# Output matmuls of a chunked S5 scan: swapping the stationary and the moving operand, on four column strips

## Chip, cores and metric

The kernel runs on one core of one Trainium2 chip. The metric is the device time of one execution in microseconds: 1356.96 us before the change, the median of three runs (1354.83 to 1357.64).

## What is computed

Two identical layers of a decoder trunk over 256 tokens of 1024 channels. Each layer has a gated feed-forward half-step, three token mixers that share one input projection, a gated merge, and a second feed-forward half-step. The change touches mixer B, an S5 layer: 32 groups of 16 channels, each with 64 complex states.

```python
def s5_layer(u, lam_re, lam_im, log_dt, b_re, b_im, c_re, c_im, d_skip):
    ...
    lam_bar = jnp.exp(lam * dt)
    b_bar = ((lam_bar - 1.0) / lam)[:, :, None] * b
    bu = jnp.einsum('gpc,bsgc->bsgp', b_bar, u32.astype(jnp.complex64))
    ...
    _, states = lax.associative_scan(combine, (a, bu), axis=1)
    y = jnp.einsum('gcp,bsgp->bsgc', c, states).real + d_skip * u32
    ...
y_b = jax.nn.gelu(s5_layer(...))
y_b = (y_b @ s5_glu_a[l]) * jax.nn.sigmoid(y_b @ s5_glu_b[l])
```

## The kernel before

**The whole.** Activations lie on 128 partitions, in two tiles of 128 tokens. Weights stream from HBM in units of 512 KB (`raw`, issued on SP at L210); ScalarE rounds each to a high part `wh` (L221), and DVE or GpSimd makes the low part `wl` from the rest (L228, L230). Each projection is three matmuls per block on these parts (`mm3`, L106 to L108), which I call wide matmuls: 128x128 stationary, 256 columns moving. A layer is one feed-forward, `mix1`, `mix2`, one feed-forward.

**What sets the order.** The program is written as one stream; the tile framework's scheduler sorts each engine's instructions by priority and by a simulated timeline, so instructions of several steps are mixed on an engine. At run time each engine works through its own list in order. `mix1` steps three Python generators in turn: `gA` (sparse attention), `gC` (dilated attention) and `gS`, the S5 layer, in between the projections.

**The S5 part.** The 256 tokens are cut into 32 chunks of eight. The 32 groups are handled in four quarters of eight groups. For a quarter q:

- `ahead(q)` and `late(q)` load what the setup (`setup_s5_layer`, during the feed-forward before) left in DRAM: `At`, the tables `tab`, the chunk inputs `U`; and `Gt` (from chunk state to outputs, L904) and `Tt` (from inputs of a chunk to its outputs, L907).
- `enter(q)` makes the chunk states: eight matmuls (L922), a rotation, a scan over the chunks on DVE (L931), a rotation back. Its last step (L937) leaves the states in `v`, 128 partitions (64 real and 64 imaginary parts) by 8 groups x 32 chunks.
- `leave(q)` makes the outputs of a quarter in one PSUM tile `yT` (tag `y`): eight matmuls of `Tt` with `U` (L944) and eight of `Gt` with the states one chunk back (L946). `Tt` and `Gt`, 128x128 per group, are the stationary operand, the 32 chunks of a group the moving one. The result stands with (position in the chunk, channel) on the 128 partitions and (group, chunk) along the columns.
- Then follows what I call the tail: Square on ScalarE (L950), two DVE operations (L951, L952), Tanh (L953), a DVE operation that makes `t1` (L954), the high part `yo` by a copy on ScalarE (L955), the low part on DVE (L956). Eight writes to DRAM (`yd`, L958, on SP) and two reads (`back`, L963) bring it to the layout that `mix2` multiplies.

L922, L944 and L946 are fp32 matmuls; the trace shows two records for each that is written. In the setup, L614 and L616 make the kernel tables `Kd` with stationary operands of 32 columns that write to 32 partitions each:

```python
for part in range(2):
    for a in range(4):
        ...
        o = pk[32 * a:32 * a + 32, 128 * s:128 * s + 128]
        ...
            PE.matmul(o[:, 16:], lh, h4[:, g, 0:7].rearrange("p n c -> p (n c)"), start=True, stop=True)
```

Attention brings transposes (L820, the 128x128 identity stationary) and matmuls with 64 stationary columns (L849, L874) into the same stage.

Of the kernel before, what the change touches and what calls it, by code (L numbers as in the profile page):

```python
# [23 lines left out]
F32 = mybir.dt.float32  # L24
F32R = mybir.dt.float32r
BF16 = mybir.dt.bfloat16
AF = mybir.ActivationFunctionType
ALU = mybir.AluOpType
AX = mybir.AxisListType

P = 128
# [41 lines left out]
def _body(ctx, tc, nc, I, out, depth, dbg):  # L73
# [7 lines left out]
    def sb(shape, dt, tag, bufs=1):  # L81
        cnt[0] += 1
        return pool.tile(shape, dt, name=f"{tag}_{cnt[0]}", tag=tag, bufs=bufs)

    def tb(shape, dt, tag, bufs=1):
        cnt[0] += 1
        return scope[-1].tile(shape, dt, name=f"{tag}_{cnt[0]}", tag=tag, bufs=bufs)
# [11 lines left out]
    def ps(tag):  # L99
        cnt[0] += 1  # L100
        return psum.tile([P, 1024 if tag == "sc" else 512], F32, name=f"{tag}_{cnt[0]}", tag=tag, bufs=PB[tag])

    V, A, G, PE = nc.vector, nc.scalar, nc.gpsimd, nc.tensor
# [10 lines left out]
    ident = sb([P, P], F32, "ident")  # L114
# [580 lines left out]
    def mix1(l, h, big, yAh, yAl, yGh, yGl):  # L695
# [48 lines left out]
        for t in range(2):  # L744
# [12 lines left out]
            for i in range(2):  # L757
# [4 lines left out]
            g = gqk[:, l:l + 1]  # L762
            A.activation(kk2[:, 0, tks[t]], pt[:, 0:P], AF.Copy, scale=g)
            V.scalar_tensor_tensor(kk2[:, 1, tks[t]], pt[:, 0:P], g, kk2[:, 0, tks[t]].bitcast(F32),
                                   op0=ALU.mult, op1=ALU.subtract)
# [132 lines left out]

        def s5():
            st = {}  # L900

            def late(q):
                Gt, Tt = tb([P, 8, 128], F32, "s5G"), tb([P, 8, 128], F32, "s5T")
                nc.sync.dma_start(Gt.rearrange("p g e -> p (g e)"), Gd[:, q])  # L904
                kq = Kd[8 * q:8 * q + 8]
                for r in range(8):
                    nc.sync.dma_start(Tt[r::8], kq[:, :, r:r + 8, :].rearrange("g x n c -> x g (n c)"))  # L907
                return Gt, Tt

            nxt = {}  # L910

            def ahead(q):
                nxt[q] = sb([P, 1024], F32, "x0"), tb([P, 3, 256], F32, "tab"), tb([P, 8, 32], F32, "s5U", 2)
                nc.sync.dma_start(nxt[q][0], Ad[:, q])
                nc.sync.dma_start(nxt[q][1], td[:, q])
                nc.sync.dma_start(nxt[q][2], ud[q].rearrange("(g c) (r k) -> (c r) g k", c=16, r=8))

            def enter(q):
                At, tab, U = nxt.pop(q)
                bu = ps("p2")  # L920
                for g in range(8):
                    PE.matmul(bu[:, 32 * g:32 * g + 32], At[:, P * g:P * g + P], U[:, g], start=True, stop=True)  # L922
                X = bu[:, :256]
                sw = tb([P, 256], F32, "s5sw")
                for e in range(2):
                    A.activation(sw[hps[e]], X[hps[1 - e]], AF.Copy)
                v, w = tb([P, 256], F32, "s5v", 2), tb([P, 256], F32, "s5w", 2)
                V.tensor_tensor(v, X, tab[:, 0], op=ALU.mult)
                V.tensor_tensor(w, sw, tab[:, 1], op=ALU.mult)
                V.tensor_tensor(v, v, w, op=ALU.subtract)  # L930
                V.tensor_tensor_scan(v, tab[:, 2], v, 0.0, op0=ALU.mult, op1=ALU.add)  # L931
                sw = tb([P, 256], F32, "s5sw")
                for e in range(2):
                    A.activation(sw[hps[e]], v[hps[1 - e]], AF.Copy)
                V.tensor_tensor(v, v, tab[:, 0], op=ALU.mult)
                V.tensor_tensor(w, sw, tab[:, 1], op=ALU.mult)
                V.tensor_tensor(v, v, w, op=ALU.add)  # L937
                st[q] = U, v

            def leave(q, Gt, Tt):  # L940
                U, v = st.pop(q)
                yT = ps("y")
                for g in range(8):
                    PE.matmul(yT[:, 32 * g:32 * g + 32], Tt[:, g], U[:, g], start=g == 0, stop=False)  # L944
                for g in range(8):
                    PE.matmul(yT[:, 32 * g + 1:32 * g + 32], Gt[:, g], v[:, 32 * g:32 * g + 31], start=False, stop=g == 7)  # L946
                yv = yT[:, :256]
                t1 = tb([P, 256], F32, "s5w", 2)
                yo = tb([P, 2, 256], F32R, "s5y")
                A.activation(t1, yv, AF.Square)  # L950
                V.tensor_scalar(t1, t1, 0.044715, 1.0, op0=ALU.mult, op1=ALU.add)  # L951
                V.tensor_tensor(t1, yv, t1, op=ALU.mult)  # L952
                A.activation(t1, t1, AF.Tanh, scale=math.sqrt(2 / math.pi))  # L953
                V.scalar_tensor_tensor(t1, t1, 1.0, yv, op0=ALU.add, op1=ALU.mult)  # L954
                A.activation(yo[:, 0], t1, AF.Copy, scale=0.5)  # L955
                V.scalar_tensor_tensor(yo[:, 1], t1, 0.5, yo[:, 0].bitcast(F32), op0=ALU.mult, op1=ALU.subtract)  # L956
                for r in range(8):
                    nc.sync.dma_start(yd[q].rearrange("i (g c) (r k) -> r c (i g) k", c=16, r=8)[r],  # L958
                                      yo[16 * r:16 * r + 16].bitcast(F32).rearrange("p i (g k) -> p (i g) k", k=32))

            def back(q):
                for i, a in enumerate((yGh, yGl)):
                    nc.sync.dma_start(a[:, q].bitcast(F32), yd[q, i])  # L963

            ahead(0)
            GT = late(0)
            for q in range(5):
                if q < 4:
                    enter(q)
                    yield  # L970
                if q > 0:
                    leave(q - 1, *GT)
                if q < 3:
                    ahead(q + 1)
                if q > 0:
                    if q < 4:
                        GT = late(q)
                    if q > 1:
                        back(q - 2)
                    yield  # L980
            back(3)
# [10 lines left out]
        gA = piped([(0, 0), (1, 0), (1, 1)], A1, A2)  # L992
        gC = attn_C()
        gS = s5()

        steps = iter([1, 0, 1, 0, 1, 0] + [1, 0, 1] + [1, 0, 1, 0, 1, 0, 1, 0] + [1] * 4)
# [143 lines left out]
    with Phase():  # L1140
        table(AF.Silu)
        with tc.high_priority():
# [5 lines left out]
            g = tb([P, D], F32, "G", 1)  # L1148
# [67 lines left out]
```

## Time and profile before

| | |
|---|---|
| median of three runs | 1356.96 us |
| the profiled execution | 1357.2 us |
| its span in the trace | 1355.4 us |
| TensorE busy | 1331.6 us (98%) |
| DVE, ScalarE, GpSimd busy | 826.8, 699.8, 465.3 us |
| mean granted clock of TensorE | 0.996 |
| DMA | 265.68 MB, 196 GB/s |

The span is the time between the first and the last instruction of the profiled execution; the rest of its 1357.2 us lies around it. Busy time of TensorE is counted from records whose ends are modelled and which overlap; where one matmul follows another, the distance of their starts is the cost. The feed-forwards fill more than half of the span; `mix1` lies from about 222 to 440 us in layer 0 and from about 890 to 1108 us in layer 1. The `leave` calls of layer 0 stand at 294 to 298, 332 to 337, 360 to 365 and 379 to 385 us, and those of layer 1 at 963, 1001, 1029 and 1048 us.

### The profile page before, as it was taken

The numbers are of one execution on the slowest core, as the hardware profiler recorded it, in microseconds if no ns is written. First come the engines' busy times: TensorE is split into PE (matmuls) and PEld (weight loads), VectorE is DVE, ScalarE is ACT, GpSimd is POOL, SyncE is SP. The second block draws the span as 40 slices with busy tenths as digits, with TensorE's granted clock in tenths as the row PEclk, the third lists the DMA queues.
The fourth block names the chain that finished last, engine by engine and source line by source line (L and its number), as shares of the span: only waits on it lengthen the run. The fifth ranks groups of instructions, "written<-read, shape, count | busy, mean of one in ns | idle before, by whom it ended". The sixth has DMA issues, their size and how long they took to land.

```text
span 1355.4 us, 25390 instructions
## 1 busy us (share of the span) xinstructions
PE 1331.6 (98%) x10120; PEld 1256.8 (93%) x10120; DVE 826.8 (61%) x1172; ACT 699.8 (52%) x1020; POOL 465.3 (34%) x333
## 2 busy tenths in 40 slices
PE   8999999999999999999999999999999999999998
PEld 7999988999999989999999999889999999899997
DVE  5696755996433665444675586569864337544443
ACT  5444445677644544444544444457766355544442
POOL 1442565454246531111122247254532555111110
PEclk9999999999999999999999999999999999999999
DMA  8866688666657556666756677766766576466662
GB/s 249 224 188 214 223 267 235 198 184 191 184 134 226 172 171 204 186 187 187 236 154 203 202 231 240 243 201 176 194 193 178 157 221 194 155 188 186 186 187 94
DMA packets 246326, 265.68 MB, mean 196 GB/s; under 512 B 51136, under 2 KB 224192, under 8 KB 246208
## 3 DMA queue, kind: packets, MB, share of 16 engines
q1 hardware_dynamic: 244400, 260.40, 64.7%
q10 hardware_dynamic: 1808, 3.67, 0.8%
q8 instruction: 79, 1.29, 0.4%
q14 instruction: 39, 0.32, 0.1%
HBM read 244.92 MB, written 18.58 MB: 194 GB/s over the span
## 4 chain that ended last, share of the span: by engine, by line
PE 76%; DVE 9%; DMA 7%; POOL 3%; ACT 2%; issue 2%; SPq 0%; ACTq 0%; DVEq 0%; POOLq 0%
PE mm L108 17%; PE mm L106 17%; PE mm L107 17%; PE pt L108 3%; PE pt L107 3%; PE pt L106 3%; DVE wl L228 3%; PE sc L108 3%; PE sc L107 3%; PE sc L106 3%; DMA raw<-in_w_in_dram 2%; DMA raw<-in_ffn_down_dram 1%; DMA raw<-in_ffn_gate_dram 1%; DMA raw<-in_ffn_up_dram 1%; PE pt L820 1%
## 5 line engine op out<-in xcount | busy, mean ns | idle before, releaser
L228 DVE TENSOR_TENSOR wl<-raw,wh 128x1024 fp32r<-128x1024 f32 (+3 forms) x376 | 443.5, 1186 | 340.8 <-ACT wh L221 327.2
L221 ACT ACTIVATE wh<-raw 128x1024 fp32r<-128x1024 f32 (+2 forms) x396 | 414.2, 1048 | 453.8 <-PE mm L107 240.8
L108 PE MATMUL mm<-hTh,wl 128*128 128x256 f32 x1728 | 490.7, 284 | 0.0
L107 PE MATMUL mm<-hTl,wh 128*128 128x256 f32 x1728 | 490.7, 284 | 0.0
L106 PE MATMUL mm<-hTh,wh 128*128 128x256 f32 x1728 | 489.0, 283 | 0.0
L106 PEld LDWEIGHTS mm<-hTh,wh 128*128 128x128 f32 x1728 | 326.5, 189 | 2.2
L108 PEld LDWEIGHTS mm<-hTh,wl 128*128 128x128 f32 x1728 | 325.9, 189 | 0.6 <-issue 0.3
L107 PEld LDWEIGHTS mm<-hTl,wh 128*128 128x128 f32 x1728 | 325.2, 188 | 1.3 <-issue 0.3
L371 POOL TENSOR_TENSOR al<-aa,ah 128x512 fp32r<-128x512 f32 x40 | 71.3, 1781 | 456.8 <-ACT ah L370 456.8
L230 POOL TENSOR_TENSOR wl<-raw,wh 128x384 fp32r<-128x384 f32 (+2 forms) x108 | 144.9, 1347 | 174.7 <-ACT wh L221 142.3
L106 PE MATMUL mm<-wh,hTh 128*128 128x256 f32 (+1 forms) x496 | 142.9, 290 | 0.0
L107 PE MATMUL mm<-wl,hTh 128*128 128x256 f32 (+1 forms) x496 | 141.8, 288 | 0.0
L108 PE MATMUL mm<-wh,hTl 128*128 128x256 f32 (+1 forms) x496 | 140.6, 288 | 0.0
L107 PEld LDWEIGHTS mm<-wl,hTh 128*128 128x128 f32 x496 | 94.1, 190 | 1.2 <-issue 0.3
L106 PEld LDWEIGHTS mm<-wh,hTh 128*128 128x128 f32 x496 | 94.0, 190 | 1.1 <-issue 0.3
L108 PEld LDWEIGHTS mm<-wh,hTl 128*128 128x128 f32 x496 | 93.1, 189 | 1.0 <-issue 0.3
L225 POOL TENSOR_TENSOR wl<-raw,wh 128x512 fp32r<-128x512 f32 x40 | 56.5, 1434 | 53.7 <-ACT wh L221 48.4
L107 PE MATMUL pt<-wl,ah 128*128 128x512 f32 x144 | 56.4, 392 | 0.0
L108 PE MATMUL pt<-wh,al 128*128 128x512 f32 x144 | 56.4, 391 | 0.0
L108 PE MATMUL sc<-wh,al 128*128 128x512 f32 x144 | 56.3, 391 | 0.0
L106 PE MATMUL pt<-wh,ah 128*128 128x512 f32 x144 | 56.2, 390 | 0.0
L107 PE MATMUL sc<-wl,ah 128*128 128x512 f32 x144 | 56.1, 390 | 0.0
(311 smaller groups left out, 2074.7 us busy)
## 6 DMA issues: line engine op xcount, KB each, us to landing
raw<-in_w_in_dram SPq DMA_DIRECT2D x100, 512.0 KB, 4.3
raw<-in_ffn_gate_dram SPq DMA_DIRECT2D x88, 512.0 KB, 4.4
raw<-in_ffn_up_dram SPq DMA_DIRECT2D x88, 512.0 KB, 4.7
raw<-in_ffn_down_dram SPq DMA_DIRECT2D x88, 512.0 KB, 4.3
raw<-in_w_out_dram SPq DMA_DIRECT2D x16, 512.0 KB, 4.2
Gd<-xh SPq DMA_DIRECT2D x8, 512.0 KB
Ad<-xl SPq DMA_DIRECT2D x8, 512.0 KB, 5.6
x<-Ad SPq DMA_DIRECT2D x8, 512.0 KB, 5.3
```

The source lines that it names most:

```text
L106: PE.matmul(o, lh, rh, start=start, stop=False)
L107: PE.matmul(o, lh, rl, start=False, stop=False)
L108: PE.matmul(o, ll, rh, start=False, stop=stop)
L221: A.activation(hv, r, AF.Copy)
L225: G.tensor_tensor(lv[:, :, cs], r[:, :, cs], hv[:, :, cs].bitcast(F32), op=ALU.subtract)
L228: V.tensor_tensor(lv[:, :, :c], r[:, :, :c], hv[:, :, :c].bitcast(F32), op=ALU.subtract)
L230: G.tensor_tensor(lv[:, :, c:], r[:, :, c:], hv[:, :, c:].bitcast(F32), op=ALU.subtract)
L371: G.tensor_tensor(al, a, ah.bitcast(F32), op=ALU.subtract)
L820: PE.transpose(pt[:, i * P:(i + 1) * P], s[:, (b0 + i) * P:(b0 + i + 1) * P], ident)
```

## The change

The states of a quarter are written to one of two tiles `Sx` with 33 columns per group, the first of them zero (four memsets on GpSimd per kernel, two per layer), so that column k holds the state ahead of chunk k. In `leave`, `U` and `Sx` become the stationary operand, 32 columns per group; `Tt` and `Gt` become the moving one, 128 columns. Four groups write to the four strips of 32 partitions of `yT`, two rounds of four fill 256 columns. The result now has (group, chunk) on the partitions and (position, channel) along the columns. The tail up to `t1` is as before; then two transposes on TensorE bring `t1` to the other half of `yT`, and the high and low part are made from there. `s5v` and `s5w` have one buffer in place of two.

```diff
+            Sx2 = [tb([P, 8, 33], F32, f"s5S{i}") for i in range(2)]
+            for Sx in Sx2:
+                G.memset(Sx[:, :, 0:1], 0.0)
...
-                v, w = tb([P, 256], F32, "s5v", 2), tb([P, 256], F32, "s5w", 2)
+                v, w = tb([P, 256], F32, "s5v"), tb([P, 256], F32, "s5w")
...
-                V.tensor_tensor(v, v, w, op=ALU.add)
-                st[q] = U, v
+                V.tensor_tensor(Sx2[q % 2][:, :, 1:], v.rearrange("p (g k) -> p g k", g=8), w.rearrange("p (g k) -> p g k", g=8), op=ALU.add)
+                st[q] = U
 
             def leave(q, Gt, Tt):
-                U, v = st.pop(q)
+                U, Sx = st.pop(q), Sx2[q % 2]
                 yT = ps("y")
-                for g in range(8):
-                    PE.matmul(yT[:, 32 * g:32 * g + 32], Tt[:, g], U[:, g], start=g == 0, stop=False)
-                for g in range(8):
-                    PE.matmul(yT[:, 32 * g + 1:32 * g + 32], Gt[:, g], v[:, 32 * g:32 * g + 31], start=False, stop=g == 7)
+                for s in range(2):
+                    for i in range(2):
+                        for a in range(4):
+                            g = 4 * s + a
+                            PE.matmul(yT[32 * a:32 * a + 32, P * s:P * s + P], (U[:, g], Sx[:, g, :32])[i], (Tt, Gt)[i][:, g],
+                                      start=i == 0, stop=i == 1)
                 yv = yT[:, :256]
-                t1 = tb([P, 256], F32, "s5w", 2)
+                t1 = tb([P, 256], F32, "s5w")
...
-                A.activation(yo[:, 0], t1, AF.Copy, scale=0.5)
-                V.scalar_tensor_tensor(yo[:, 1], t1, 0.5, yo[:, 0].bitcast(F32), op0=ALU.mult, op1=ALU.subtract)
+                for s in range(2):
+                    PE.transpose(yT[:, 256 + P * s:256 + P * s + P], t1[:, P * s:P * s + P], ident)
+                A.activation(yo[:, 0], yT[:, 256:], AF.Copy, scale=0.5)
+                V.scalar_tensor_tensor(yo[:, 1], yT[:, 256:], 0.5, yo[:, 0].bitcast(F32), op0=ALU.mult, op1=ALU.subtract)
```

The scheduler sorts `mix1` anew from quarter 0's `leave` on; the rest of the program keeps its order. Three places show how. Names end in a number of the tile; a stationary operand stands last in a matmul's row, and "x4" means four such rows on end.

TensorE, quarter 0's `leave` in layer 0, before: the matmuls of `Tt` (L944) are split by one set of attention transposes (L820).

```order
L108 MATMUL mm_3529<-wh_3422,hTl_2393 128x256
L944 MATMUL y_3636<-s5U_3133,s5T_3138 128x32 x2
L820 MATMUL pt_3365<-ident_67,att_s_3086 128x128 x4
L944 MATMUL y_3636<-s5U_3133,s5T_3138 128x32 x6
L946 MATMUL y_3636<-s5v_3160,s5G_3137 128x31 x8
L106 MATMUL mm_3687<-wh_3429,hTh_2392 128x256
```

The same place now (the new matmuls are L950):

```order
L108 MATMUL mm_3533<-wh_3426,hTl_2393 128x256
L950 MATMUL y_3640<-s5T_3142,s5U_3137 32x128 x3
L820 MATMUL pt_3369<-ident_67,att_s_3086 128x128 x4
L950 MATMUL y_3640<-s5T_3142,s5U_3137 32x128
L950 MATMUL y_3640<-s5G_3141,s5S_524_3131 32x128 x4
L950 MATMUL y_3640<-s5T_3142,s5U_3137 32x128 x4
L950 MATMUL y_3640<-s5G_3141,s5S_524_3131 32x128 x4
L106 MATMUL mm_3693<-wh_3433,hTh_2392 128x256
```

The 16 matmuls stand in two pieces in both; in the other quarters they now stand in four, two and three pieces. Behind this place stood 13 wide matmuls before the next step of attention (L849), and now 32.

DVE, the tail of quarter 1 in layer 0, before: L951, L952 and L954 make `t1`, L956 the low part, L801 belongs to attention, L228 makes the low part of a weight.

```order
L951 TENSOR_SCALAR s5w_4061<-s5w_4061 128x256
L952 TENSOR_TENSOR s5w_4061<-y_4044,s5w_4061 128x256
L801 ISA att_s_4120,sm_689_4127<-sc_4119,cm_66 128x384
L954 SCALAR_TENSOR_TENSOR s5w_4061<-s5w_4061,y_4044 128x256
...
L956 SCALAR_TENSOR_TENSOR s5y_4062<-s5w_4061,s5y_4062 128x256
L228 TENSOR_TENSOR wl_4262<-raw_3988,wh_4261 128x4x160
```

And now (L956, L957 and L959 make `t1`, L963 the low part):

```order
L956 TENSOR_SCALAR s5w_4067<-s5w_4067 128x256
L957 TENSOR_TENSOR s5w_4067<-y_4050,s5w_4067 128x256
L801 ISA att_s_3972,sm_665_3979<-sc_3971,cm_66 128x384
...
L959 SCALAR_TENSOR_TENSOR s5w_4067<-s5w_4067,y_4050 128x256
...
L826 TENSOR_TENSOR yAl_2477<-pt_3791,yAh_2476 128x2x128
L801 ISA att_s_4128,sm_691_4135<-sc_4127,cm_66 128x384
...
L963 SCALAR_TENSOR_TENSOR s5y_4068<-y_4050,s5y_4068 128x256
L228 TENSOR_TENSOR wl_4270<-raw_3994,wh_4269 128x4x160
```

Two steps of attention (L826, L801) now stand between `t1` and the low part, and a weight's low part still stands behind it.

ScalarE, the tail of quarter 3 in layer 0, before: three weights are rounded (L221) behind the copy L955.

```order
L950 ACTIVATE s5w_4653<-y_4636 128x256
L953 ACTIVATE s5w_4653<-s5w_4653 128x256
L955 ACTIVATE s5y_4654<-s5w_4653 128x256
L221 ACTIVATE wh_4740<-raw_4604 128x1024
L221 ACTIVATE wh_4774<-raw_4672 128x512
L221 ACTIVATE wh_4809<-raw_4707 128x1024
```

And now (L958 is Tanh, L962 the copy, which reads the transposes):

```order
L958 ACTIVATE s5w_4663<-s5w_4663 128x256
L221 ACTIVATE wh_4752<-raw_4614 128x1024
L962 ACTIVATE s5y_4664<-y_4646 128x256
L221 ACTIVATE wh_4786<-raw_4684 128x512
L221 ACTIVATE wh_4821<-raw_4719 128x1024
```

One of the weights moved ahead of the copy, the two others stay behind it. On TensorE, 37 wide matmuls and three of 64 columns (L874) stand between this quarter's last output matmul and its transposes.

## Rows read from the trace of the kernel before

**Rows 1.** The page, part 1: busy time, share of the span and instructions of each engine.

```profile
PE 1331.6 (98%) x10120; PEld 1256.8 (93%) x10120; DVE 826.8 (61%) x1172; ACT 699.8 (52%) x1020; POOL 465.3 (34%) x333
```

**Rows 2.** Stretches of layer 0: from:to, length, busy of PE, PEld, DVE, ACT, POOL; clock.

```profile
300.00:360.00 60.00, 59.63 (x516) 56.50 (x515) 38.92 (x85) 41.63 (x80) 21.66 (x14) 1.00 0.68 186
400.00:440.00 40.00, 40.00 (x340) 40.00 (x339) 15.70 (x17) 19.17 (x23) 26.41 (x20) 1.00 0.71 211
```

**Rows 3.** Chain that ended last, quarters 2 and 3 of layer 0: start, us, what.

```profile
362.30 1.03 PE y L944 x10
363.33 1.79 PE y L946 x16
...
379.66 0.36 PE y L944 x4
...
381.49 1.46 PE y L944 x12
382.94 1.78 PE y L946 x16
```

**Rows 4.** Instructions of L946: durations in ns (min/median/max), first and last start.

```profile
L946 PE MATMUL y<-s5v,s5G x128: 275/275/276, 296.6 to 1052.8; 128*128 128x31 f32 x128
```

**Rows 5.** Timeline of TensorE in the setup: start us, us, instruction and form.

```profile
133.22 0.28 PE L108 MATMUL mm<-hTh,wl 128*128 128x256 f32 x1
133.43 0.32 PE L616 MATMUL y<-s5C,xh 128*32 128x16 f32 x8
133.57 0.41 PE L614 MATMUL y<-xh,xh 128*32 128x112 f32 x8
133.80 0.26 PE L616 MATMUL y<-s5C,xh 128*32 128x16 f32 x8
133.89 0.41 PE L614 MATMUL y<-xh,xh 128*32 128x112 f32 x8
134.23 0.39 PE L106 MATMUL mm<-hTh,wh 128*128 128x256 f32 x1
134.46 0.28 PE L107 MATMUL mm<-hTl,wh 128*128 128x256 f32 x1
```

**Rows 6.** Timeline of TensorE around two attention transposes in layer 0.

```profile
374.95 0.28 PE L108 MATMUL mm<-hTh,wl 128*128 128x256 f32 x1
375.07 0.38 PE L820 MATMUL pt<-ident,att_s 128*128 128x128 f32 x2
...
375.41 0.28 PE L107 MATMUL mm<-hTl,wh 128*128 128x256 f32 x1
```

**Rows 7.** Stretches behind quarter 2 in both layers, columns as in rows 2.

```profile
365.00:368.00 3.00, 3.00 (x17) 3.00 (x17) 0.72 (x2) 1.97 (x5) 0.00 (x0) 0.53 1.03 265
368.00:371.00 3.00, 3.00 (x29) 2.87 (x30) 1.89 (x5) 1.87 (x4) 0.00 (x0) 0.90 0.71 219
...
1032.00:1035.00 3.00, 3.00 (x25) 3.00 (x25) 0.81 (x3) 2.66 (x6) 0.00 (x0) 0.87 0.77 218
1035.00:1038.00 3.00, 3.00 (x17) 3.00 (x17) 1.37 (x4) 1.52 (x5) 0.00 (x0) 0.56 0.87 232
```

**Rows 8.** Timelines of ScalarE and DVE: the tails of quarters 0 and 3.

```profile
298.96 0.38 ACT L950 ACTIVATE s5w<-y 128x256 f32<-128x256 f32 x1
303.05 0.42 DVE L954 SCALAR_TENSOR_TENSOR s5w<-s5w,y 128x256 f32<-128x256 f32 x1 [0.48 <-ACT s5w L953]
384.76 0.38 ACT L950 ACTIVATE s5w<-y 128x256 f32<-128x256 f32 x1 [2.95 <-PE y L946]
386.49 0.42 DVE L954 SCALAR_TENSOR_TENSOR s5w<-s5w,y 128x256 f32<-128x256 f32 x1 [0.48 <-ACT s5w L953]
```

**Rows 9.** Waits of TensorE, 255 to 420 us: total us, times, longest.

```profile
PE pt L849 <- DVE cq L721: 0.4, 1, 0.4
```

**Rows 10.** Timelines of DVE and TensorE: a weight of branch C made and read.

```profile
391.16 0.49 DVE L228 TENSOR_TENSOR wl<-raw,wh 128x320 fp32r<-128x320 f32 x1 [1.58 <-ACT wh L221]
396.09 0.28 PE L106 MATMUL pt<-kk,wh 128*128 128x256 f32 x1
```

## The prediction

> **What bounds the kernel now.** I read the page's engine totals first: TensorE is busy 98% of the span [rows 1]. An average over stages can hide where that holds, so I read the windows next. In the stage where the change sits, from about 300 to 440 us in layer 0, TensorE is busy 59.63 of 60 us and then 40.00 of 40 us, while DVE is busy 38.92 and 15.70, ACT 41.63 and 19.17, and the DMA engines carry 0.68 and 0.71 [rows 2]. There a microsecond taken from TensorE should be a microsecond of the kernel, unless something that was late only by a little takes over.
>
> The chain of waits shows the code itself on the path. In quarter 3 of layer 0 the `leave` matmuls hold 0.36 + 1.46 us (L944) and 1.78 us (L946), 3.60 us in all [rows 3]. The form says why: L946 has 128 records over eight quarters, so 16 for the eight matmuls written (each fp32 matmul is two records), with a stationary operand of 128x128 and 31 moving columns [rows 4]. 16 records in 1.78 us are 0.111 us each; where only projections run, 340 records with 256 columns take 40.00 us, 0.118 us each [rows 2]. So the narrow ones pay the same pace for an eighth of the columns: the load of 128 columns sets it.
>
> **The change, part by part.**
>
> *Removed:* 32 records per quarter, 3.60 us [rows 3], eight quarters in two layers: 28.8 us.
>
> *Added, the matmuls:* again 16 written, 32 records, but with 32 stationary columns on four column strips and 128 moving ones. The trace of before has nearly this form, in the setup's matmuls at L614 and L616 [rows 5]: four strips of 32 columns, fp32, the same order over the strips, 16 records with 112 moving columns and 16 with 16. They stand between ordinary matmuls: L108 starts at 133.22 and would be followed at 133.34; the next L106 starts at 134.23, so 0.89 us, and the one behind that comes 0.23 us later in place of 0.12, another 0.11 us [rows 5]. That is 1.00 us for 32 records. For the wider moving operand: the first L616 block takes 0.14 us (133.43 to 133.57) and the first L614 block 0.23 us, so 96 more columns cost 0.09 us for eight records. Two blocks grow by 112 columns (0.105 us each) and two by 16 (0.015 us each): 0.24 us. I take 1.24 us per quarter, 9.9 us in all. The bounds are 1.00 us (the columns hide) and 32 x 0.111 = 3.6 us (the strips don't run side by side); L614 is nearest by far, being the same form.
>
> *Breaks:* the order shows the 16 matmuls of a quarter in 2, 4, 2 and 3 pieces, with transposes and attention matmuls between. That is 7 more entries per layer than one run each. Entering cost 133.43 - 133.34 = 0.09 us and leaving 0.11 us [rows 5], so 14 x 0.20 = 2.8 us, an upper value, as some neighbours are column-split themselves; nothing is the lower one.
> The Trainium skill ("TensorEngine Tiling (Array Packing)", Key Properties) says that changing the tiling mode drains TensorE, which speaks against cutting the work into pieces; it gives no time. The 0.20 us above agrees with it.
>
> *Added, the transposes:* two per quarter, 16. Two such (L820) between wide matmuls stretch 374.95 to 375.41, 0.46 us where two wide starts take 0.24, so 0.22 us for two [rows 6]; 1.8 us in all.
> The Trainium skill ("TensorE: Matmul & The Clock Gate", Part 4: PE-mode transpose) gives about 275 ns for a transpose in a kernel. By that figure 16 would cost 4.4 us and the sum end at 1343.1; the trace has them overlap, so I keep 1.8.
>
> *The clock:* the granted clock falls to half twice, 0.53 in 365 to 368 and 0.56 in 1035 to 1038 [rows 7]. Lost: 3 x (0.47 + 0.10) = 1.7 us in layer 0 and 3 x (0.13 + 0.44) = 1.7 us in layer 1. The first comes right behind quarter 2's `leave`, 2.8 us of narrow matmuls on end from 362.30 to 365.12 [rows 3]; quarter 2 of layer 1 ends there too. That run becomes about 1 us. But quarter 3's, 3.2 us on end from 381.49 [rows 3], brought no fall, so the run alone doesn't decide. I count both falls as gone, 3.4 us; the bounds are that they stay (0) and that each of eight `leave`s brings one (below).
>
> *The vector tail:* Square, the two DVE operations, Tanh and the last DVE operation stay as they are; the copy and the subtraction read PSUM in place of SBUF, same shapes. The add at L937 writes rows of 33. Four memsets on GpSimd are new, which is busy 21.66 of 60 us. I put all this at nothing: DVE and ACT idle about a third of the stage [rows 2], and operations of this shape that read PSUM today, L950 with 0.38 us and L954 with 0.42, take what the copy and the subtraction take [rows 8]. If that cover were gone, the eight tails would be on the path at some 0.4 us per operation that has grown.
>
> *The new wait:* the transposes sit in TensorE's queue and need the tail's t1. Queued behind them are the projections, so a late t1 stops everything. From Square to the end of t1 takes 386.49 + 0.42 - 384.76 = 2.2 us in quarter 3 and 303.05 + 0.42 - 298.96 = 4.5 us in quarter 0 [rows 8]; Square starts right behind the matmuls, which end at 384.72 [rows 3]. The order puts 37 wide matmuls and three half-wide ones between quarter 3's last matmul and its transposes, 37 x 0.12 + 0.3 = 4.7 us; the same count gives 5.1 us in quarter 1, 6.1 in quarter 2 and about 9 in quarter 0. Each cover is about twice its need, so I count no wait. Behind the transposes ACT's copy and DVE's subtraction come some 2.7 us later than now (4.7 + 0.2 + two of 0.4 behind the matmuls, for 2.2 and two of 0.4), the weight conversions queue behind those on ACT and DVE, and SP's write of `yd` with weight loads behind it. The tightest weight there is ready at 391.65 and its low part is read 0.24 us behind the start at 396.09, 4.7 us of cover [rows 10]; 2.7 us fit.
>
> *What is late next:* behind quarter 0 TensorE already waits 0.4 us for DVE's L721 [rows 9]. The new order gives it 32 wide matmuls before that point where 13 stood, so the time freed is filled from further on. I give back 0.5 us per layer, 1.0 us.
>
> *Sum:* -28.8 + 9.9 + 2.8 + 1.8 - 3.4 + 1.0 = -16.7 us. The profiled execution was 1357.2 us (0.24 above the median of 1356.96, so nothing is corrected): **1340.5 us**.
>
> **The rivals.** *The clock falls stay.* Around quarter 2 attention transposes and short matmuls stand too, and those remain. Then 3.4 us are not won: 1343.9 us. For it speaks quarter 3, whose longer run brought none; against it, that the falls stand behind the same quarter in both layers [rows 7].
> *The clock falls behind every `leave`.* Transposes and 32-column tiles might count for less than what they replace: eight falls for two, 8 x 1.7 = 13.7 us in place of none: 1354.2 us. Against it: the clock is 1.00 from 300 to 360 us [rows 2], where quarter 1's `leave` and many transposes stand.
> The Trainium skill ("TensorE: Matmul & The Clock Gate", Part 4) says that transposes don't count as a busy TensorE in the way matmuls do; by that rule this rival holds. The trace bears it out little, by the same row.
> *DVE paces quarter 0.* If the order's filling fails there, both quarters 0 are lost, 2 x (3.60 - 1.24 - 0.20 - 0.22) = 3.9 us: 1344.4 us.
> *The strips run one after another* (slower). Then 256 records at the pace of 0.111 us cost 28.4 us, the breaks 2.8, the transposes 1.8, and the clock stays: +4.2 us, 1361.4 us. It decides from (28.8 - 2.8 - 1.8) / 256 = 0.095 us per record; L614 shows 0.03. For it speaks only that no row shows four strips with 128 moving columns each.
>
> **How the numbers follow.** Forecast 0.60; falls stay 0.20; DVE paces 0.10; falls behind every `leave` 0.04; one after another 0.05; the rest 0.01. Range: below, no cost of breaks, no wait and 1.00 us per quarter: 1340.5 - 2.8 - 1.0 - 1.9 = 1334.8; above, falls that stay and quarter 0 lost: 1340.5 + 3.4 + 3.9 = 1347.8, with a microsecond for the tail's cover. I take 1335 to 1349. A measurement of this kernel tells 0.2% (2.7 us) from no change. All cases up to 1344.4 are faster; the one at 1354.2 lies on the bound and is halved: faster 0.92, the same 0.03, slower 0.05.
>
> **What would show it.** In the profile after: the `leave` matmuls' starts at 0.03 to 0.05 us each, not 0.11; no granted clock near 0.5 in the two stretches; no wait of TensorE for t1 at the transposes; TensorE still busy throughout 300 to 430 us. Idle time of TensorE there, with a wait on DVE or on a weight, would make the give-back larger; a pace of 0.1 us per record would turn the sign.

## The result, and the profile after

The changed kernel takes 1342.32 us (median of 4 executions, 1341.03 to 1344.03), the kernel before on the same chip 1357.03 us (4 executions, 1354.83 to 1357.64): a ratio of 0.9899, 95% interval 0.9881 to 0.9916, so faster by about 1%. The prediction had 1340.5 us in 1335 to 1349. The profiled execution took 1342.03 us, 15.2 us less than the one of before.

The page's engine totals show where it went. The row, as in [rows 1]:

```profile
PE 1317.1 (98%) x10136; PEld 1235.7 (92%) x10136; DVE 829.7 (62%) x1172; ACT 699.2 (52%) x1020; POOL 457.3 (34%) x337
```

TensorE lost 14.5 us of busy time (1331.6 to 1317.1) with 16 records more, and still fills 98% of the span. So what TensorE saved, the kernel saved. The stretches of [rows 2] and [rows 7], with the same columns:

```profile
300.00:360.00 60.00, 59.94 (x550) 55.08 (x548) 41.59 (x86) 44.65 (x85) 18.40 (x15) 1.00 0.70 194
400.00:440.00 40.00, 40.00 (x340) 40.00 (x339) 14.91 (x15) 18.53 (x22) 25.10 (x20) 1.00 0.70 221
365.00:368.00 3.00, 3.00 (x39) 2.83 (x36) 1.59 (x5) 2.97 (x7) 1.65 (x1) 1.00 0.92 259
368.00:371.00 3.00, 3.00 (x29) 3.00 (x27) 0.66 (x2) 1.70 (x3) 0.28 (x1) 1.00 0.94 269
1032.00:1035.00 3.00, 3.00 (x33) 2.31 (x33) 0.49 (x1) 1.78 (x4) 1.16 (x2) 1.00 0.57 126
1035.00:1038.00 3.00, 3.00 (x47) 2.34 (x43) 1.05 (x3) 0.63 (x2) 1.20 (x1) 1.00 0.43 129
```

TensorE is as full as before, and the granted clock is 1.00 in every one of them: both falls are gone from this execution. The waits of TensorE from 255 to 425 us (total us, times, longest) are one row, a wait that before has too (1.5 us there); that of [rows 9] is gone, and none at the new transposes has come:

```profile
PE pt L656 <- DVE qn L652: 1.6, 2, 1.0
```

The matmuls and the transposes by line (durations in ns, first and last start), which answers to [rows 4]:

```profile
L950 PE MATMUL y<-s5T,s5U x128: 272/273/297, 294.7 to 1036.2; 128*32 128x128 f32 x128
L950 PE MATMUL y<-s5G,s5S x128: 272/273/298, 295.6 to 1036.5; 128*32 128x128 f32 x128
...
L961 PE MATMUL y<-ident,s5w x16: 271/272/327, 307.0 to 1042.0; 128*128 128x128 f32 x16
```

(In these rows, as in those of L820, the data is the stationary operand and the identity the moving one, not the other way round.) One strip record still lasts as long as an old one (273 ns against 275); what has changed is how many run at a time. That shows in their starts. TensorE's timeline around quarter 2's `leave`, where [rows 3] had 1.03 + 1.79 us and more:

```profile
357.56 0.28 PE L108 MATMUL mm<-hTh,wl 128*128 128x256 f32 x1
357.77 0.42 PE L950 MATMUL y<-s5T,s5U 128*32 128x128 f32 x6
358.12 0.39 PE L860 MATMUL sc<-ck,cq 128*128 128x256 f32 x1
358.35 0.28 PE L861 MATMUL sc<-ckl,cq 128*128 128x256 f32 x1
...
358.81 0.28 PE L861 MATMUL sc<-ckl,cq 128*128 128x256 f32 x1
359.02 0.30 PE L950 MATMUL y<-s5T,s5U 128*32 128x128 f32 x1
...
359.59 0.48 PE L950 MATMUL y<-s5G,s5S 128*32 128x128 f32 x5
360.01 0.38 PE L106 MATMUL mm<-yAh,wh 128*128 128x256 f32 x1
360.23 0.28 PE L107 MATMUL mm<-yAl,wh 128*128 128x256 f32 x1
```

Six records in one piece and 26 in another, 0.35 and 0.99 us: 1.34 us for the quarter in place of 3.6. The rows also show what the pieces cost. The record ahead of a piece stands 0.21 us (357.56 to 357.77, 358.81 to 359.02) and the one behind it 0.22 (360.01 to 360.23) where 0.12 is usual.

I matched the projection records (L106) of the two traces by their number and followed the difference of their starts. It goes from +0.2 to -7.2 us across layer 0's stage and by another -7.4 across layer 1's; outside them two steps of -1.2 and +0.6 us remain. The stages' 14.8 us are what the steps below have to explain; the two steps come back with either sign, up to about 1 us, between other executions of these kernels too, so I put them to no cause.

### The profile page after: what moved, and what is told of

The parts are those of the page before. It is cut to its first block, busy times and chain, and to the rows that moved or that the text cites. A ratio compares the mean times of both kernels' runs of the same rounds, so it can differ in the third digit from the quotient of the medians.

```text
span 1340.2 us, 25446 instructions
## 1 busy us (share of the span) xinstructions
PE 1317.1 (98%) x10136; PEld 1235.7 (92%) x10136; DVE 829.7 (62%) x1172; ACT 699.2 (52%) x1020; POOL 457.3 (34%) x337
## 4 chain that ended last, share of the span: by engine, by line
PE 76%; DMA 7%; DVE 6%; POOL 4%; ACT 3%; issue 2%; SPq 1%; ACTq 0%; DVEq 0%; POOLq 0%
PE mm L106 18%; PE mm L108 18%; PE mm L107 18%; PE pt L107 3%; PE pt L108 3%; PE pt L106 3%; PE sc L108 2%; PE sc L107 2%; PE sc L106 2%; DVE wl L228 2%; DMA raw<-in_w_in_dram 2%; DMA raw<-in_ffn_down_dram 2%; ACT wh L221 1%; PE pt L820 1%; PE y L950 1%
## 5 line engine op out<-in xcount | busy, mean ns | idle before, releaser
L228 DVE TENSOR_TENSOR wl<-raw,wh 128x1024 fp32r<-128x1024 f32 (+3 forms) x376 | 446.5, 1194 | 331.0 <-ACT wh L221 328.1
L221 ACT ACTIVATE wh<-raw 128x1024 fp32r<-128x1024 f32 (+2 forms) x396 | 414.3, 1049 | 450.0 <-PE mm L107 238.9
L107 PE MATMUL mm<-hTl,wh 128*128 128x256 f32 x1728 | 490.6, 284 | 0.0
L106 PE MATMUL mm<-hTh,wh 128*128 128x256 f32 x1728 | 489.7, 283 | 0.0
L106 PEld LDWEIGHTS mm<-hTh,wh 128*128 128x128 f32 x1728 | 326.5, 189 | 3.2 <-issue 1.1
L107 PEld LDWEIGHTS mm<-hTl,wh 128*128 128x128 f32 x1728 | 325.2, 188 | 1.0
L230 POOL TENSOR_TENSOR wl<-raw,wh 128x384 fp32r<-128x384 f32 (+2 forms) x108 | 137.9, 1282 | 169.0 <-ACT wh L221 152.3
L106 PE MATMUL mm<-wh,hTh 128*128 128x256 f32 (+1 forms) x496 | 142.9, 290 | 0.3 <-ACT hTh L282 0.3
L107 PE MATMUL mm<-wl,hTh 128*128 128x256 f32 (+1 forms) x496 | 142.2, 289 | 0.1
L106 PEld LDWEIGHTS mm<-wh,hTh 128*128 128x128 f32 x496 | 94.1, 190 | 1.4 <-ACT hTh L282 0.5
L107 PEld LDWEIGHTS mm<-wl,hTh 128*128 128x128 f32 x496 | 94.1, 190 | 1.3 <-issue 0.3
L107 PE MATMUL pt<-wl,ah 128*128 128x512 f32 x144 | 56.4, 392 | 0.0
L106 PE MATMUL pt<-wh,ah 128*128 128x512 f32 x144 | 56.2, 390 | 0.0
L107 PE MATMUL sc<-wl,ah 128*128 128x512 f32 x144 | 56.1, 390 | 0.0
```

What stands on the lines that cost most here:

```text
L106: PE.matmul(o, lh, rh, start=start, stop=False)
L107: PE.matmul(o, lh, rl, start=False, stop=False)
L221: A.activation(hv, r, AF.Copy)
L228: V.tensor_tensor(lv[:, :, :c], r[:, :, :c], hv[:, :, :c].bitcast(F32), op=ALU.subtract)
L230: G.tensor_tensor(lv[:, :, c:], r[:, :, c:], hv[:, :, c:].bitcast(F32), op=ALU.subtract)
```

## The experiments

**Strip by strip.** Do the strips really work at one time, or are the records cheap because a stationary operand of 32 columns is small?

```
-for s in range(2):
-    for i in range(2):
-        for a in range(4):
+for a in range(4):
+    for s in range(2):
+        for i in range(2):
```

> The changed kernel with one edit: the loops of the leave matmuls run strip by strip (the four products of one strip behind each other), so that four neighbouring matmuls no longer stand on four strips. Theory: the 0.027 us per record come from four strips that work at one time, so strip by strip a record costs at least the moving time of its 128 columns, half of the 0.118 us that 256 columns take, 0.059 us: 256 x (0.059 - 0.027) = +8 us, about 1350 us; up to 256 x (0.111 - 0.027) = +21 us, about 1363 us, if the load sets the pace as in the kernel before. Rival: it is the narrower stationary operand (32 columns in place of 128) that made the records cheap, whatever their order: 1342.3 us unchanged.

Measured: 1351.83 us (8 executions, 1349.56 to 1354.76). Quarter 2's second piece in TensorE's timeline:

```profile
364.64 0.42 PE L950 MATMUL y<-s5T,s5U 128*32 128x128 f32 x4
364.88 0.39 PE L950 MATMUL y<-s5G,s5S 128*32 128x128 f32 x4
365.11 0.41 PE L950 MATMUL y<-s5T,s5U 128*32 128x128 f32 x4
...
366.05 0.38 PE L950 MATMUL y<-s5T,s5U 128*32 128x128 f32 x2
366.26 0.38 PE L950 MATMUL y<-s5G,s5S 128*32 128x128 f32 x2
366.58 0.39 PE L106 MATMUL mm<-yAh,wh 128*128 128x256 f32 x1
```

Four records take 0.23 us, 0.058 each, against 0.027 in the changed kernel. By the starts of L106 the two stages are 8.7 us longer than there (9.5 us by the medians), near the 8 expected: the order decides. But the reason is not the one expected. A strip's own records stand in the order T T G G T T G G, so four of T and then four of G are two strips at work at one time: while one strip does its last four records, the next strip does its first four beside it. The last four records of the piece, behind which no other strip comes, show a strip by itself: 0.21 us for two (366.05 to 366.26), 0.109 each by their starts. That is as slow as the old form's 0.111. So nothing is won per record by turning the operands round alone; all of it comes from strips at one time, two here, four in the changed kernel (0.109 / 4 = 0.027). The 0.059 of the expectation, half of a projection record's 0.118, was met by chance: a strip's record with 128 columns takes 0.109.

**The pieces, put together.** All quarters first, then all but quarter 0.

```
+with tc.high_priority():
     for s in range(2):
```

> The changed kernel with one edit: the 16 leave matmuls of a quarter get the scheduler's high priority, so that they stand in one piece (quarter 0 in two), earlier in TensorE's queue, in place of 2, 4, 2 and 3 pieces. Theory: each extra piece costs about 0.37 us of TensorE (0.09 at the entry, 0.17 because the last record is drained, 0.10 at the exit, read in the trace of the changed kernel). One extra piece is left of seven in each layer, so 12 x 0.37 = 4.4 us are won: about 1338 us. By the prediction's 0.20 us it would be 12 x 0.20 = 2.4 us: about 1340 us. Rival: the pieces cost nothing of their own, what the stage lost lies elsewhere: 1342.3 us as the changed kernel, or slower if the matmuls, now earlier in the queue, wait for their inputs (an idle time of TensorE ahead of them, ended by DVE or ACT).

Measured: 1341.18 us (5 executions, 1337.51 to 1342.49; 0.9868 of before, interval 0.9845 to 0.9891). Little was won, and the waits of TensorE from 255 to 425 us say why:

```profile
PE y L951 <- DMA s5U<-ud: 1.6, 1, 1.6
PE pt L820 <- DVE x L728: 1.0, 1, 1.0
```

2.6 us of idle time in layer 0 is as much as one layer's six pieces were to bring: quarter 0's matmuls had come ahead of their input's DMA, and the attention waits for DVE. In layer 1 TensorE stands 1.7 us ahead of the same matmuls, and right behind that this execution has two falls of the clock (0.63 from 920 to 923 us and 0.60 from 927 to 930): the new matmuls don't rule falls out. So the priority was kept for quarters 1 to 3:

```
+with tc.high_priority() if q else ExitStack():
     for s in range(2):
```

> The changed kernel with one edit: the 16 leave matmuls of quarters 1 to 3 get the scheduler's high priority and stand in one piece; quarter 0 is as in the changed kernel. In the run with all four quarters early, TensorE stood 1.6 us in quarter 0 ahead of these matmuls, for the DMA of U, and the attention's L820 waited 1.0 us. Theory: six extra pieces go in each layer, 12 x 0.37 = 4.4 us, without that wait: about 1338 us. By the prediction's 0.20 us per piece: 2.4 us, about 1340 us. Rival: pieces cost nothing on the path, 1342.3 us.

Measured: 1339.26 us (4 executions, 1338.12 to 1341.51; 0.9872 of before, interval 0.9854 to 0.9890). The changed kernel beside it in the same runs, unedited:

> The changed kernel once more, unedited, beside the same runs of the kernel before: about 1342 us, and a mean granted clock over the span of 0.996 to 0.997 in every execution, where the kernel before shows 0.987 to 0.999. Theory: the old matmuls bring falls of the clock, of changing number and place, and the new ones few. Rival: the two kernels differ in this by chance only; then the changed kernel shows executions at 0.99 too, some 4 us longer.

Measured: 1343.67 us (4 executions, 1342.60 to 1344.25; 0.9902, interval 0.9886 to 0.9918), with a clock of 0.994 to 0.997. So the 12 pieces were worth 4.4 us, as the theory had it. TensorE's timeline of quarter 1 in the version with whole quarters:

```profile
336.56 0.29 PE L107 MATMUL mm<-hTl,wh 128*128 128x256 f32 x1
336.68 0.28 PE L108 MATMUL mm<-hTh,wl 128*128 128x256 f32 x1
336.89 0.43 PE L951 MATMUL y<-s5T,s5U 128*32 128x128 f32 x8
337.14 0.40 PE L951 MATMUL y<-s5G,s5S 128*32 128x128 f32 x8
337.36 0.40 PE L951 MATMUL y<-s5T,s5U 128*32 128x128 f32 x8
337.57 0.40 PE L951 MATMUL y<-s5G,s5S 128*32 128x128 f32 x8
337.91 0.77 PE L849 MATMUL pt<-att_pt,av 128*64 128x128 f32 x10
```

32 records from 336.89 to 337.91 are 1.02 us. With 0.09 at the entry and 0.10 at an exit into wide matmuls that is 1.21 us per quarter; the prediction had 1.24. The matmuls' own price was right. By the starts of L106 in the profiled executions each stage is 2.1 us shorter than in the changed kernel: 4.2 / 12 = 0.35 us per piece.

The same version once more, in other runs:

> The version with quarters 1 to 3 in one piece once more, to see whether its gain over the changed kernel holds: 4.4 us below it, about 1339 us. Rival: the 4.4 us of the first time were partly chance (the start of the program differs by up to 3 us between executions); then 1341 to 1342 us.

Measured: 1336.58 us (5 executions, 1332.08 to 1340.09; 0.9858 of before, interval 0.9833 to 0.9884). It beats both kernels; its interval and that of the changed kernel touch at the edges, but next to each other their executions (1338.12 to 1341.51 and 1342.60 to 1344.25) don't overlap.

**Three breaks by themselves.** The same instructions in the same quarter 0, three small transposes (of which nothing reads the result) once between the blocks of strips, as here, once all three behind the loops.

```
+dm = ps("p2")
 for s in range(2):
     for i in range(2):
+        if s + i:
+            PE.transpose(dm[:, :P], ident, ident)
         for a in range(4):
...
```

> The run with quarters 1 to 3 in one piece, with three 128x128 transposes of the identity added per quarter (nobody reads them). In quarter 0 they stand between the four blocks of four strip matmuls, three extra breaks; in the other quarters the scheduler puts all three elsewhere. Read against the next run in quarter 0 of each layer, from the first strip matmul to the projection behind the last: theory 3 x 0.37 = 1.1 us longer there, by the prediction's price 3 x 0.20 = 0.6 us, if breaks cost nothing 0.

> The same with the three added transposes of quarter 0 behind its four blocks in place of between them: the same instructions, three breaks fewer. The difference to the run before it in that stretch is the price of three breaks: theory 1.1 us, the prediction 0.6 us.

Measured, one execution each (1339.81 and 1339.72 us). TensorE's timeline of quarter 0 with the transposes between the blocks:

```profile
295.27 0.41 PE L954 MATMUL y<-s5T,s5U 128*32 128x128 f32 x2
295.61 0.33 PE L951 MATMUL p<-ident 128*128 128x128 f32 x1
295.87 0.43 PE L954 MATMUL y<-s5G,s5S 128*32 128x128 f32 x8
296.22 0.33 PE L951 MATMUL p<-ident 128*128 128x128 f32 x1
296.48 0.43 PE L954 MATMUL y<-s5T,s5U 128*32 128x128 f32 x8
296.84 0.33 PE L951 MATMUL p<-ident 128*128 128x128 f32 x1
297.10 0.42 PE L954 MATMUL y<-s5G,s5S 128*32 128x128 f32 x8
297.45 0.39 PE L106 MATMUL mm<-wh,hTh 128*128 128x256 f32 x1
297.68 0.28 PE L107 MATMUL mm<-wl,hTh 128*128 128x256 f32 x1
```

and behind them:

```profile
294.58 0.30 PE L952 MATMUL y<-s5T,s5U 128*32 128x128 f32 x1
...
295.15 0.48 PE L952 MATMUL y<-s5G,s5S 128*32 128x128 f32 x5
295.57 0.55 PE L955 MATMUL p<-ident 128*128 128x128 f32 x3
295.87 0.36 PE L106 MATMUL mm<-wh,hTh 128*128 128x256 f32 x1
296.07 0.27 PE L107 MATMUL mm<-wl,hTh 128*128 128x256 f32 x1
```

From the first record to L107 it is 297.68 - 295.27 = 2.41 us against 296.07 - 294.58 = 1.49: three breaks cost 0.92 us, 0.31 each (0.92 in layer 1 too). That lies between the theory's 1.1 and the prediction's 0.6 for the three, nearer the theory. Of each break 0.11 us is the last record of the piece, which stands 0.20 us before the next instruction starts, where in one piece the next block starts 0.09 behind it; another 0.16 is the transpose, which stands 0.26 us (295.61 to 295.87) in place of 0.10. The two whole times are equal all the same: in the second version TensorE then waits ahead of quarter 1's matmuls, 0.8 us for DVE in layer 0 and 0.2 us for a DMA in layer 1, and the first has neither wait. The price holds where TensorE is full, and this pair doesn't show it in the kernel's time.

**The transposes.** Left out of the changed kernel:

```
-for s in range(2):
-    PE.transpose(yT[:, 256 + P * s:256 + P * s + P], t1[:, P * s:P * s + P], ident)
-A.activation(yo[:, 0], yT[:, 256:], AF.Copy, scale=0.5)
-V.scalar_tensor_tensor(yo[:, 1], yT[:, 256:], 0.5, yo[:, 0].bitcast(F32), op0=ALU.mult, op1=ALU.subtract)
+A.activation(yo[:, 0], t1, AF.Copy, scale=0.5)
+V.scalar_tensor_tensor(yo[:, 1], t1, 0.5, yo[:, 0].bitcast(F32), op0=ALU.mult, op1=ALU.subtract)
```

> The changed kernel without the two transposes of a quarter: the copy and the subtraction read t1 in SBUF as in the kernel before, so the quarter's outputs stay transposed. Theory (starts in the trace): 16 transposes at 0.09 us, -1.4 us, about 1340.9 us; by the prediction 16 x 0.11 = -1.8 us, 1340.5 us. Rival: their 275 ns each count in full, or TensorE stands at them for t1: -4.4 us or more, below 1338 us.

Measured: 1341.33 us (4 executions, 1339.40 to 1342.69), 1.0 us below the changed kernel and 2.3 below its later executions (1343.67). That fits both -1.4 and -1.8 us and speaks against -4.4, but it doesn't price the transposes closely: by the starts of L106 the two stages are 3.1 us shorter, and with the edit the order has changed too (20 pieces of strip matmuls in place of 22). Then the same six lines the other way round, added to the kernel before:

> The kernel before with its own matmuls, and the two transposes of t1 per quarter added ahead of the copy and the subtraction (the quarter's outputs are then transposed). Theory: 16 transposes at 0.09 to 0.11 us, +1.4 to +1.8 us on the kernel before (about 1359 us), no wait of TensorE for t1, and a granted clock that falls as in the kernel before, mean 0.99 to 0.995. Rival: the transposes are what changes the clock; then it stays at 0.996 or above and the time comes out at or below the kernel before. Second rival: TensorE waits for t1; then +4 us or more.

Measured: 1359.39 us (10 executions, 1353.68 to 1365.76; 1.0029 of before, interval 1.0007 to 1.0051), no wait for t1. That is 2.6 us above the median of the kernel before, but its own executions spread over 12 us. The transposes by line, and the stretches of [rows 7]:

```profile
L956 PE MATMUL y<-ident,s5w x16: 271/272/329, 305.9 to 1055.1; 128*128 128x128 f32 x16
```

```profile
365.00:368.00 3.00, 3.00 (x29) 3.00 (x28) 1.13 (x3) 2.77 (x6) 0.82 (x1) 1.00 0.32 68
368.00:371.00 3.00, 3.00 (x28) 3.00 (x27) 2.02 (x5) 2.15 (x6) 0.00 (x0) 1.00 0.87 259
...
1035.00:1038.00 3.00, 3.00 (x35) 2.87 (x35) 1.55 (x5) 2.14 (x5) 0.00 (x0) 1.00 0.91 244
```

By start to next start eight transposes take 0.83 us, 0.104 each, 1.7 us in all; a wide matmul behind them takes 0.20 us in place of 0.12. This execution still has the old matmuls and yet no fall at either place. That gives the price of a fall: against it, the L106 and L820 records of the kernel before lose 1.5 us between 365.3 and 368.7 us and 1.5 us between 1034.3 and 1037.7. With these taken out, each stage is 1.1 us longer than before, 2.2 us for the 16 transposes. But it also says that the falls don't belong to the place.

**The run of narrow matmuls, cut in two.** In the kernel before, the T half of a quarter goes one step earlier:

```
+if q > 0:
+    half(q - 1, *GT)
 enter(q)
 yield
```

Here `half` issues the eight products with T, and `leave` keeps the eight with G.

> The kernel before with one edit: the eight products with T of a quarter are issued one step earlier than the eight with G, ahead of the next quarter's enter, so that no 32 narrow matmul records stand on end. Theory: the unbroken run of narrow records brings the two falls of the clock near 365 and 1034 us; with it broken the granted clock stays near 1.00 there and 3.4 us are won, about 1353.6 us. Rival: the falls hang on the number of narrow records or transposes in the whole neighbourhood, not on their being on end: two falls stay, 1357 us.

Measured: 1361.84 us (10 executions, 1355.07 to 1366.49; 1.0028 of before, interval 1.0006 to 1.0051), and the profiled execution has five falls behind its start, three of them:

```profile
283.00:286.00 3.00, 3.00 (x16) 3.00 (x15) 2.52 (x2) 2.98 (x7) 2.85 (x3) 0.50 0.41 69
351.00:354.00 3.00, 3.00 (x15) 2.42 (x14) 1.87 (x4) 0.92 (x3) 0.00 (x0) 0.54 0.87 266
...
989.00:992.00 3.00, 3.00 (x23) 2.63 (x23) 0.34 (x2) 0.38 (x1) 0.00 (x0) 0.59 0.69 189
```

The theory fell: the unbroken run is not what brings them. Nor does one profile tell how many there are: behind the start the profiled executions with the old matmuls have 2, 1 and 5, those with the new ones none to two. What does hold shows in the mean granted clock of every execution. With the old matmuls (the kernel before beside these experiments, and the last two) it was 0.993 or lower in 35 of 61; with the new matmuls, or with almost none (next), in none of 40, where the lowest was 0.994. Of the kernel before, the 12 executions at 0.995 or above have a median of 1353.6 us, all 41 one of 1356.8: the falls that the change takes away are worth some 3 us.

**Almost no `leave` matmuls.** How far does the stage follow TensorE?

```
-for g in range(8):
-    PE.matmul(yT[:, 32 * g:32 * g + 32], Tt[:, g], U[:, g], start=g == 0, stop=False)
-for g in range(8):
-    PE.matmul(yT[:, 32 * g + 1:32 * g + 32], Gt[:, g], v[:, 32 * g:32 * g + 31], start=False, stop=g == 7)
+PE.matmul(yT[:, :256], Tt[:, 0], U.rearrange("p g k -> p (g k)"), start=True, stop=False)
+PE.matmul(yT[:, :256], Gt[:, 0], v, start=False, stop=True)
```

> The kernel before with its 16 leave matmuls of a quarter replaced by two with 256 moving columns each (T and G of the first group for all groups; the outputs of the other groups are left out). Four records of about 0.12 us stand in place of 3.60 us of narrow ones: 8 x (3.60 - 0.48) = 25.0 us less on TensorE. Theory: TensorE bounds the stage throughout, all of it is won but 1 us, and the falls go with the narrow matmuls (3.4 us): about 1330 us. Rival: DVE, ACT or a weight's DMA is late soon after what the change has already freed; then it ends at 1338 us or above, with idle time of TensorE in 290 to 430 us.

Measured: 1336.27 us (4 executions, 1335.70 to 1338.22; 0.9852 of before, interval 0.9832 to 0.9872). That is 6 us short of the theory, but not for the rival's reason: the wait that [rows 9] shows has only grown from 0.4 to 0.9 us.

```profile
PE pt L820 <- DVE cq L721: 0.9, 1, 0.9
```

Part of the rest is my price for the two matmuls: with 256 fp32 columns and a stationary operand of 128 their records start 0.215 us apart, and they take 0.72 us per quarter by their starts, not 0.48, 1.9 us in all. So TensorE still bounds the stage with eleven microseconds per layer taken out (by the starts of L106). The other 4 us I have only in part: the matmuls removed and the falls were worth 0.6 and 0.4 us less than counted, and the profiled execution has a fall of the clock behind the stage, 0.63 from 1132 to 1135 us, where it loses 1.7 us against the kernel before. That wait's 1.0 us in two layers is what the theory had given back. The rest, under 2 us, stays open.

## Why the prediction was right, and where it was off

The time lies in the range, 1.8 us above the forecast. The time alone would fit the rival "the falls stay" (1343.9) as well; the trace decides for the forecast's mechanism and finds a mis-sized term that happens to move the sum the same way. By the steps of the prediction, us over both layers:

| step | predicted | measured | from |
|---|---|---|---|
| old matmuls removed | -28.8 | -28.2 | starts of L944 and L946, 14.1 per layer |
| new matmuls | +9.9 | +9.7 | 8 x 1.21, a quarter in one piece |
| breaks | +2.8 | +4.9 | 14 x 0.35, from the 12 that were taken away |
| transposes | +1.8 | +1.4 to +2.2 | 0.71 per layer by their own starts; 1.1 by the stages when added to before |
| clock falls | -3.4 | -3.0 | 2 x 1.5 |
| give-back, tail, wait | +1.0 | -0.8 | the 0.4 us of [rows 9], gone in both layers; no new wait |
| the stages | -16.7 | -16.0 to -15.2 | sum; -14.8 by the starts of L106 |

Read one by one, the terms close to about 1 us; that rest is in none of them.

**Bound.** TensorE was and stays busy throughout the stage; the saving went into the end one to one.

**Strips.** The form at L614 [rows 5] foretold the pace: the records start 0.027 us apart. The run strip by strip shows that this needs the order over the strips, and that the rival had the right price for a strip by itself (0.109 us; it had 0.111). That the two paces are so near is chance. The moving columns set the strip's: eight records, two on each strip, take 0.14 us with 16 columns and 0.23 with 112 [rows 5], and the 0.215 us of 256 fp32 columns in the run with almost no `leave` matmuls would make 0.107 for 128, an estimate. The old form moves 31 or 32 columns, so its 0.111 is not that.

**Breaks: the step that was mis-sized.** The prediction took 0.09 us for the entry and 0.11 for the exit from one place in the setup, and called 0.20 "an upper value". But there was one piece only in those rows, and its last record was counted with its matmuls. Every further piece has a last record of its own that stands 0.20 us, in place of 0.09 where the strips' round of four is complete and of 0.027 on average: 0.09 + 0.11 + 0.10 = 0.30 to 0.09 + 0.17 + 0.10 = 0.36 us, measured at 0.31 and 0.35. That is 2.1 us of the 14 breaks. The Trainium skill ("TensorEngine Tiling (Array Packing)", Key Properties) says that a change of the tiling mode drains TensorE. The runs agree, with 0.31 to 0.35 us per piece; that the slow last record is this drain is not shown.

**Falls.** They were counted as gone and are, and 3.0 us is near 3.4. The reason was only half right: their number and places change from execution to execution, so two falls behind quarter 2 in both layers were no property of quarter 2. That the two falls of one profiled execution came out near the some 3 us that the falls are worth over all executions of the kernel before is luck. The Trainium skill ("TensorE: Matmul & The Clock Gate", Part 4) says that transposes don't count as a busy TensorE in the way matmuls do. Here 16 more of them leave the clock as it is, in the kernel before (0.993 or lower in 4 of 10 executions with them, 23 of 41 without) as in the new one (in none of 8 with them, none of 4 without). Why the old matmuls bring falls that the new ones don't stays open.

**Transposes and the wait for t1.** 271 ns long each, but 0.09 to 0.10 us by their starts, and 0.08 us more for a wide matmul behind them: two come to 0.22 us, as the rows of L820 said [rows 6]. The cover of five microseconds was enough: no TensorE wait stands at L961.

**Give-back.** I gave back 1.0 us to DVE in quarter 0. The wait of [rows 9] is gone instead, in both layers: the same order that brings wide matmuls forward covered it. So this term came out 1.8 us better than forecast and hid most of the 2.1 us in the breaks: the sum is as near as it is because two errors cancel.

## What to carry to other kernels

Small matmuls that take as long for 31 columns as wide ones for 256 (0.111 and 0.118 us here) can be turned around, the small operand stationary on 32-column strips, neighbours on different strips: here 3.6 us became 1.2. A strip by itself was no faster than the old form; two at one time brought a good half of the gain, four the rest, so the order over the strips is the change. Count the pieces that a scheduler makes of such a run, and price each with its entry, its exit and its slow last record, some 0.35 us here; keeping a run together was worth a third of what the change itself brought. But move it no earlier than its inputs come, or the gain stands there again as a wait.

## What was unexpected about the hardware

- A strip's records with 128 fp32 columns start 0.109 us apart, beside three other strips (0.027 per record in all), beside one (0.058) or alone. The last one stands 0.20 where another form follows.
- The falls of the granted clock from 1.00 to 0.50 (2.4 to 1.2 GHz), worth about 1.5 us each, come at places and in a number that change between executions of one kernel. Over the executions with the old matmuls the mean clock runs from 0.987 to 0.999, and the time of the kernel before from 1352.11 to 1362.45 us. With the new matmuls the clock stays at 0.994 to 0.999.
- Matmuls of F32 operands with 256 moving columns and a full stationary operand start 0.215 us apart; those of the projections, whose operands the program types F32R, 0.118, though the profile prints one form for both.
